# TensorE's order in a decoder step: a scheduler's interleave, or the order of the text

## The chip, the cores and the metric

The kernel runs on one core of one Trainium2 chip. The time is the device time of one launch in microseconds (us), the median of several runs. Each core has a TensorE for matrix products (PE in the profile; its weight loads are PEld), VectorE (DVE) and ScalarE (ACT) for elementwise work, GpSimd (POOL), SyncE (SP), and 16 DMA engines. Each engine runs its own list of instructions in the order in which the built program holds them, and waits for the others by semaphores. So the order in which the instructions of one engine stand is itself part of a kernel.

## The reference

One inference step of a two-layer trunk of width 1024, for a prompt of 1024 tokens and a sample group of 8 x 8 tokens, all in fp32:

```
for layer in (0, 1):
    h = rmsnorm(x)
    layer 0: a_h, a_b, a_c, a_z, shift_in, b_z = split(h @ w_in)
             y_a = a_b * conv3(a_c * a_h) * silu(a_z)
             r, k, v, wl, al = token_shift(shift_in)
             S_t = S_{t-1} * w_t - (S_{t-1} kk_t)(kk_t a_t)^T + v_t k_t^T
             y_b = (group_norm(S_t r_t) + bonus) * silu(b_z)
    layer 1: windowed means with a matrix per group; a gated MLP over chunks of 128 tokens
    x = x + concat(two branches) @ w_out
y = rmsnorm(x)
```

The recurrence S_t has 8 heads of 64 x 64. It is computed in chunks of 64 tokens, by products of 64 x 64 matrices and the inverse of a triangular matrix for each head and chunk.

## The kernel before

The 1088 tokens are the columns of every product. They go in three blocks: block 0 has the 64 sample tokens and 256 of the prompt (320 columns), blocks 1 and 2 have 384 each. Weights come from DRAM in pieces of 128 x 512, and are split into a high part (`whi`, ScalarE, L145) and a low part (`wlo`, VectorE, L146), with 4 buffers of each; activations are split the same way into `hi` and `lo`. A dense product of 1024 inputs and 128 outputs (`product`, L157) is three matmuls for each of 8 steps of 128 inputs: L162 (`hi,whi`), L163 (`lo,whi`) and L164 (`hi,wlo`), 24 in all. I call 12 of them a half: one half uses one piece of the weights. Layer 0 has 33 products of input projection per block (66 halves: 17 products for the recurrence's branch and the gate, then 16 for the convolution branch) and 8 of output projection (16 halves); halves are numbered through the program from 0, and layer 0 has 246.

Between the dense products of layer 0 stand small ones, in three kinds of work per block. *Preparation* (`rwkv_prep`) runs per group of 128 tokens (two chunks), and once for the sample group, nine groups in all: two low-rank products (L487, L488), sums of squares (L496), a spread by transposes (L521), and then on VectorE and ScalarE the decays `Pp`, their inverses `iP`, and the scaled operands. `AR` holds a and r, `BK` holds b and k; in each the second index is the slot. Their products (L555) give `GT`. *Inverse* (`rwkv_inverse`): 31 steps of two VectorE instructions (L610, L612) over all chunks of the block together, and then the result goes through DRAM (L614, L619, L632). *Recurrence* (`recur`): the merge of the inverse's two halves (L639, L651), then for each chunk `chunk_parts` (b and k turned by products with the identity, L692), `rwkv_chunk` (L761 to L788), and for each group the group norm and `group_out` (turned back at L732, result `yr` to DRAM at L739). The output projection (`out_proj0`) reads `yr` from DRAM.

What sets the order. The Tile scheduler orders all engines by its own estimate and by priorities. The kernel bounds it on TensorE: `later()` chains each product behind the one before, `marks` records the last matmul of each half, and `recur` runs its generators (the merge, the chain, the sample, and the preparation of the next block) under `issue_after(marks[...])`, so that a step may start from a certain half on, at 0.7 halves a step (0.5 for the preparation). Where in the dense stream a small product stands from there on is for the scheduler.

Of the kernel before, what the change touches and what calls it, by code (L numbers as in the profile page):

```python
# [8 lines left out]
ALU = mybir.AluOpType  # L9
# [9 lines left out]
AT = (10, 10, 0)  # L19
EARLY, RATE, PREP_RATE = 20, 0.7, 0.5  # L20
# [53 lines left out]
def build(nc, tc, a):  # L74
    from contextlib import ExitStack
    ctx = ExitStack()

# [72 lines left out]
    order, marks = {}, []  # L150

    def later():

        return tc.issue_after(order["last"]) if order else ExitStack()

    def product(ps, w, h, c0, n):

        with later():
            for k in range(KT):
                wh, wl = w[k // 4]  # L160
                hh, hl = h[k]
                mm(ps, wh[:, k % 4, :], hh[:, c0:c0 + n], start=k == 0, stop=False)  # L162
                mm(ps, wh[:, k % 4, :], hl[:, c0:c0 + n], start=False, stop=False)  # L163
                i = mm(ps, wl[:, k % 4, :], hh[:, c0:c0 + n], start=False, stop=k == KT - 1)  # L164
# [61 lines left out]
    def raw_h(B):  # L226
# [32 lines left out]
        with urgent():  # L259
            token_rstd(acc, n, B.ms0, pc, "pp", 4)  # L260
            spread_rstd(B.ms0, n, ev, pc, "pp", "d", XTs[2].rearrange("p a b -> p (a b)"), 4)
            B.rstd = XTs[2].rearrange("p a b -> p (a b)")[:, :n]
            B.rstd2 = XTs[1].rearrange("p a b -> p (a b)")[:, :n]
            act(B.rstd2, B.rstd, AF.Square)
        return h
# [16 lines left out]
    def rms_token(B):  # L282
        B.ms0 = mk(ev, [128, 4], "rms_m", 2)
        with later():
            token_rstd(B.acc, B.n, B.ms0, pd, "dn")

    def rms_spread(B):
        with later():
            B.rstd = spread_rstd(B.ms0, B.n, ev, pd, "dn")
# [175 lines left out]
    def rwkv_prep(B, t0, T, g):  # L465
# [17 lines left out]

        ap, lw = pp(), pp()
        for p in range(4):
            s = slice(p * T, (p + 1) * T)
            mm(ap[:, s], wa2[64:128, p * 128:(p + 1) * 128], B.S28[64:128, cols], start=True, stop=True)  # L487
            mm(lw[:, s], wa2[0:64, p * 128:(p + 1) * 128], B.tw[:, cols], start=True, stop=True)  # L488
        for p in range(4):
            act(sb[:, p], ap[:, p * T:(p + 1) * T].rearrange("p (c s) -> p c s", c=ng_), AF.Tanh,  # L490
                bias=a0h[:, p:p + 1], scale=0.5)
# [37 lines left out]
        for p in range(4):  # L529
            act(g4(kp)[:, p], sb[:, p], AF.Identity, scale=kah[:, p:p + 1], bias=kah1[:, p:p + 1])  # L530
        tt(v3(kp), v3(kp), B.KS[:, :, cols], ALU.mult)
        if g is None:
            stt(sb[:, :, 0, :], sb[:, :, 0, :], 1.0, v3(kkn), ALU.add, ALU.mult)
        else:
            sb2 = sb.rearrange("p a c s -> p (a c) s")
            stt(sb2, sb2, 1.0, kkn.rearrange("p (a s) -> p a s", s=64), ALU.add, ALU.mult)
        yield
        tt(m4(sb), m4(sb), iP, ALU.mult)  # L538
        tt(m4(sa), kv4, Pp[:, :, :, 0:Lc], ALU.mult)
        yield  # L540
        tt(m4(sk), kp.rearrange("p (a c s) -> p a c s", a=4, c=nc_), iP, ALU.mult)
# [4 lines left out]
        for c in range(ng_):  # L546
# [134 lines left out]
    def chunk_parts(B, g, c):  # L681
# [6 lines left out]
        for p in range(4):  # L688
            for q in range(2):
                for e in range(2):  # L690
                    r = slice(64 * e, 64 * e + 64)
                    mm(bps[e][64 * q:64 * q + 64, p * 64:(p + 1) * 64], B.BK[g][r, p, c, q ^ e, :], ident[r, r],  # L692
                       start=True, stop=True)
# [47 lines left out]
    def rwkv_chunk(B, g, c, parts, yps):  # L741
# [23 lines left out]
        first = state.get("y")  # L765
# [615 lines left out]
```

## Time and profile before

| | |
|---|---|
| runs | 1135.46, 1141.45, 1141.25 us, median 1141.25 |
| the profiled execution, its time | 1138.01 us |
| its span | 1136.2 us |
| TensorE busy | 1090.4 us, 96% |
| VectorE, ScalarE, GpSimd busy | 729.5, 491.5, 164.4 us |
| mean granted TensorE clock | 0.967 |

The span is the time from the first to the last instruction, the run has 1.8 us around it. Shares of busy time are means over stretches of different kinds, so the rows below go by stretches and places. A matmul counts as busy also while the clock is granted at half, and while it stands between others that it keeps apart.

### The profile page before, as it was taken

The page shows a single profiled execution, that of the slowest core. Times are in us where ns is not written, and L with a number is a line of the kernel's source. Part 1 is how long each engine was busy: PE and PEld are TensorE (multiplying, and loading weights), DVE is VectorE, ACT ScalarE, POOL GpSimd, SP SyncE. Part 2 cuts the span into 40 slices and gives each one's busy share as a digit, 9 for nine tenths or more (in the row PEclk, how much of TensorE's full clock was granted, in tenths as well). Part 3 has the DMA queues.
Part 4 walks back from the last instruction along what each step waited for, and adds up shares of the span by engine and source line. Part 5 has one row for each costly group of instructions (what it writes and reads, how often), then busy time and mean ns, then how long its engine had stood idle before and what let it go on. Part 6 is the DMA issues. An engine that isn't in the chain of part 4 may idle for free.

```text
span 1136.2 us, 22856 instructions
## 1 busy us (share of the span) xinstructions
PE 1090.4 (96%) x8719; PEld 1003.7 (88%) x8719; DVE 729.5 (64%) x1526; ACT 491.5 (43%) x1017; POOL 164.4 (14%) x282
## 2 busy tenths in 40 slices
PE   7999999999999999999899999999999999999996
PEld 6998999876756899878799889899999999999995
DVE  7878899457632799478797477695373442245456
ACT  6376654365412554666535654464212111133232
POOL 2313343110301212113301011001010100000000
PEclk9999999899966999999999999899999999999998
DMA  8464563554412454535545687775201111112455
GB/s 263 149 212 129 157 206 123 146 157 145 128 58 65 121 189 125 140 104 150 155 152 149 185 242 222 228 254 186 79 21 55 38 48 38 53 41 91 116 154 183
DMA packets 135341, 154.91 MB, mean 136 GB/s; under 512 B 45560, under 2 KB 88696, under 8 KB 135232
## 3 DMA queue, kind: packets, MB, share of 16 engines
q1 hardware_dynamic: 130912, 146.36, 41.8%
q0 software_dynamic: 2256, 5.03, 2.2%
q10 hardware_dynamic: 2064, 2.08, 0.6%
q8 instruction: 68, 1.11, 0.4%
q14 instruction: 41, 0.34, 0.1%
HBM read 127.77 MB, written 25.64 MB: 135 GB/s over the span
## 4 chain that ended last, share of the span: by engine, by line
PE 40%; DVE 5%; DMA 4%; issue 1%; ACT 1%; POOL 1%; SPq 0%; DVEq 0%; ACTq 0%; POOLq 0%
PE dn L162 12%; PE dn L163 12%; PE dn L164 12%; DMA xn<-xd 2%; DVE wlo L146 1%; PE pl L1166 1%; DVE lo L171 1%; PE pl L1230 1%; DMA wraw<-wout 1%; DVE xn L1071 1%; POOL gvs L712 0%; DMA ma<-yd 0%; ACT whi L145 0%; DMA ma<-yr 0%; PE pp L732 0%
## 5 line engine op out<-in xcount | busy, mean ns | idle before, releaser
L162 PE MATMUL dn<-hi,whi 128*128 128x384 f32 (+1 forms) x1648 | 557.4, 338 | 12.9 <-ACT whi L145 6.5
L163 PE MATMUL dn<-lo,whi 128*128 128x384 f32 (+1 forms) x1648 | 551.9, 335 | 0.4 <-DVE lo L171 0.2
L164 PE MATMUL dn<-hi,wlo 128*128 128x384 f32 (+1 forms) x1648 | 551.5, 335 | 0.3 <-DVE wlo L146 0.3
L145 ACT CAST whi<-wraw 128x512 fp32r<-128x512 f32 x326 | 201.0, 619 | 347.1 <-PE dn L163 287.9
L162 PEld LDWEIGHTS dn<-hi,whi 128*128 128x128 f32 x1648 | 314.5, 191 | 25.2 <-ACT whi L145 6.9
L146 DVE TENSOR_TENSOR wlo<-wraw,whi 128x512 fp32r<-128x512 f32 x326 | 223.4, 687 | 159.5 <-ACT whi L145 146.8
L164 PEld LDWEIGHTS dn<-hi,wlo 128*128 128x128 f32 x1648 | 314.4, 191 | 8.5 <-issue 5.6
L163 PEld LDWEIGHTS dn<-lo,whi 128*128 128x128 f32 x1648 | 314.9, 191 | 7.7 <-issue 3.7
L183 POOL TENSOR_TENSOR rms_m<-rms_m,nhalf 128x3 f32<-128x3 f32 (+2 forms) x8 | 6.9, 870 | 218.3 <-DVE rms_m L182 218.3
L555 PE MATMUL pp<-AR,BK 64*64 64x128 f32 x544 | 36.3, 289 | 1.9 <-DVE BK L538 1.6
L555 PEld LDWEIGHTS pp<-AR,BK 64*64 64x64 f32 x544 | 22.0, 138 | 13.9 <-issue 9.8
L612 DVE TENSOR_TENSOR iv<-iv,prod 80x31 f32<-80x31 f32 (+23 forms) x93 | 31.3, 336 | 2.0
L610 DVE TENSOR_TENSOR prod<-iv 80x31 f32<-80x31 f32 (+23 forms) x93 | 31.2, 336 | 1.8
L565 POOL DMA_DIRECT2D dl<-GT x32 | 20.3, 636 | 77.8 <-DVE GT L558 77.8
L712 POOL TENSOR_TENSOR gvs<-gvs,nhalf 128x8 f32<-128x8 f32 (+1 forms) x9 | 15.1, 1674 | 113.0 <-DVE gvs L711 100.6
L1272 DVE TENSOR_TENSOR big<-dn,x1s 128x384 f32<-128x384 f32 (+1 forms) x24 | 12.8, 534 | 27.7 <-PE dn L164 27.7
L558 DVE TENSOR_TENSOR GT<-pp,cst 128x512 f32<-128x512 f32 x34 | 22.1, 683 | 12.3 <-PE pp L555 12.3
L324 POOL COPY q<-carry 128x1 f32<-128x1 f32 x26 | 22.5, 866 | 48.5 <-DVE KS L339 19.7
L1278 ACT ACTIVATE sq<-big 128x384 f32<-128x384 f32 (+1 forms) x21 | 10.7, 508 | 35.1 <-DVE big L1272 35.0
L796 DVE TENSOR_TENSOR pch<-pch,SV 64x256 f32<-64x256 f32 x32 | 13.9, 434 | 17.9 <-PE pch L786 16.3
L500 POOL TENSOR_TENSOR rn<-rn,nhalf 128x8 f32<-128x8 f32 (+1 forms) x9 | 15.5, 1719 | 48.7 <-DVE rn L499 48.7
L326 DVE TENSOR_TENSOR d<-q 128x384 f32<-128x384 f32 (+1 forms) x39 | 20.6, 529 | 1.9 <-ACT q L320 1.5
(279 smaller groups left out, 1246.9 us busy)
## 6 DMA issues: line engine op xcount, KB each, us to landing
wraw<-win SPq DMA_DIRECT2D x246, 256.0 KB, 2.8
wraw<-wout SPq DMA_DIRECT2D x80, 256.0 KB, 3.0
x<-xT SPq DMA_DIRECT2D x48, 192.0 KB, 3.7
xd<-x SPq DMA_DIRECT2D x16, 192.0 KB, 3.1
xn<-xd SPq DMA_DIRECT2D x16, 192.0 KB, 3.9
x1s<-xd SPq DMA_DIRECT2D x16, 192.0 KB, 2.4
yT<-big SPq DMA_DIRECT2D x16, 192.0 KB, 3.7
i<-vd SPq DMA_DIRECT2D x34, 64.0 KB, 2.6
```

The lines of the kernel that those rows point to most:

```text
L145: A.copy(hi, raw)
L146: tt(lo, raw, hi.bitcast(F32), ALU.subtract)
L162: mm(ps, wh[:, k % 4, :], hh[:, c0:c0 + n], start=k == 0, stop=False)
L163: mm(ps, wh[:, k % 4, :], hl[:, c0:c0 + n], start=False, stop=False)
L164: i = mm(ps, wl[:, k % 4, :], hh[:, c0:c0 + n], start=False, stop=k == KT - 1)
L324: G.tensor_copy(q[:, 0:1], carry[:, j:j + 1])
L326: tt(d[:, :n], q[:, 0:n], q[:, 1:1 + n], ALU.subtract)
L555: mm(gp[e][o:o + 64, p * 128:(p + 1) * 128], BK[b:b + 64, p, c, q ^ (e if g is not None else 0), :], AR[b:b + 64, p, c, :, :].rearrange("p ...
L558: tt(GT[:, e::2, :], v3(gp[e]), m[e].unsqueeze(1).broadcast_to([128, 4, 128]), ALU.mult)
L565: nc.gpsimd.dma_start(of_half(B.dl[i], e), GT[64 * e:64 * e + 64, e::2, 0:64])
L610: tt(pr, X[:Q, 0:k, q:q + 1].broadcast_to([Q, k, r]), Lb[:Q, q:q + 1, k:32].broadcast_to([Q, k, r]), ALU.mult)
L612: tt(o, o, pr, ALU.add)
```

## The change

TensorE is taken out of the scheduler's hands (`manual_schedule` for this engine): its instructions stand in the order of the text. The other engines are still ordered by the scheduler. `weave` hands a generator to `half_done`, which `product` calls after each half: each generator has a half from which on it runs, and a rate in halves per step. The start points are in the text of `main`: preparation 27 halves after its block's begin at half a half per step, the recurrences 4, 8 and 4 halves after the place where they are handed over. `finish()` runs what is left.

In the preparation, the value `ta` has its own tile, and `scaled` writes b and k of the odd heads to exchanged slots (`q ^ e`), with two instructions of half the partitions instead of one of all. So in `BK` the stationary operand of a head is one piece of 128 columns: L555 with 64 x 64 operands (16 per chunk) becomes L581 with 64 x 128 (8 per chunk), and L692 becomes 8 transposes (L717).

```diff
+    ctx.enter_context(tc.manual_schedule(engines={mybir.EngineType.PE}))
...
+    def weave(gen, after=0, rate=1.0):
+        streams.append([halves[0] + after, rate, gen])
+    def step(x):
+        with tc.high_priority():
+            if next(x[2], 0) is not None:
+                streams.remove(x)
+        x[0] += x[1]
+    def half_done():
+        halves[0] += 1
+        while streams and (x := min(streams, key=lambda x: x[0]))[0] <= halves[0]:
+            step(x)
...
     def product(ps, w, h, c0, n):
-        with later():
...
-                if k in (3, 7):
-                    marks.append(getattr(i, "ins", i))
-        order["last"] = marks[-1]
+            if k in (3, 7):
+                half_done()
...
+        def scaled(x, q):
+            x = x.rearrange("p (a c s) -> p a c s", a=4, c=nc_)
+            if g is None:
+                tt(m4((sb, sk)[q]), x, iP, ALU.mult)
+            else:
+                for e in range(2):
+                    r, o = slot(e, q)
+                    tt(o, x[r], iP[r], ALU.mult)
...
-                for q in range(2):
-                    for e in range(2):
-                        o, b = 64 * q, 64 * e
-                        mm(gp[e][o:o + 64, p * 128:(p + 1) * 128], BK[b:b + 64, p, c, q ^ (e if g is not None else 0), :],
-                           AR[b:b + 64, p, c, :, :].rearrange("p a s -> p (a s)"), start=True, stop=True)
+                for e in range(2):
+                    r = slice(64 * e, 64 * e + 64)
+                    mm(gp[e][:, p * 128:(p + 1) * 128], BK[r, p, c, :, :].rearrange("p a s -> p (a s)"),
+                       AR[r, p, c, :, :].rearrange("p a s -> p (a s)"), start=True, stop=True)
...
-                    mm(bps[e][64 * q:64 * q + 64, p * 64:(p + 1) * 64], B.BK[g][r, p, c, q ^ e, :], ident[r, r],
-                       start=True, stop=True)
+                PE.transpose(bps[e][:, p * 64:(p + 1) * 64], B.BK[g][r, p, c, :, :].rearrange("p a s -> p (a s)"),
+                             ident[r, r])
...
+    weave(prep(b0), 27, 0.5)
     rwkv_in(b0)
...
+    weave(rwkv_sample(b0), 2)
     mixer_a(b0, hs[0], (3,))
     hs.append(rms_h(b1))
-    at = len(marks)
+    for x in recur(b0):
+        weave(x, 4)
+    weave(prep(b1, b0), 27, 0.5)
     rwkv_in(b1)
...
+    for x in recur(b1):
+        weave(x, 8)
+    weave(prep(b2, b1), 27, 0.5)
     rwkv_in(b2)
     mixer_a(b2, hs[2], range(4))
...
+    for x in recur(b2):
+        weave(x, 4, 0.9)
     out_proj0(b0)
     out_proj0(b1)
-    with boost(mark):
-        recur(b2, at + AT[2])
+    finish()
...
+    weave(layer_norm(), 1)
```

The rest of the diff moves what the two orders need: `rstd` of block 0 becomes a generator, the wait of the sample for its start (`now`) goes, the tiles `ys` and `prod` share a buffer, and the chaining calls `later()` and `issue_after` go from both layers.

Three places show what the order is. First, TensorE, in the input projection of block 1, where the preparation's products of one group stand; `dn` is the dense product's result, `pp` that of the small ones. Before:

```order
L164 MATMUL dn_3183<-hi_2196,wlo_3180 128x384
L555 MATMUL pp_4536<-AR_4447,BK_4446 64x128
L162 MATMUL dn_3183<-hi_2203,whi_3179 128x384
L555 MATMUL pp_4537<-AR_4447,BK_4446 64x128
L163 MATMUL dn_3183<-lo_2204,whi_3179 128x384
```

After:

```order
L178 MATMUL dn_3569<-hi_2209,wlo_3560 128x384
L176 MATMUL dn_3569<-hi_2216,whi_3559 128x384
L177 MATMUL dn_3569<-lo_2217,whi_3559 128x384
L178 MATMUL dn_3569<-hi_2216,wlo_3560 128x384
L581 MATMUL pp_3582<-AR_3439,BK_3438 128x128
L581 MATMUL pp_3583<-AR_3439,BK_3438 128x128
```

Before, most of the 32 products L555 of this group stand singly between dense matmuls; after, the 16 products L581 of a group stand behind each other, after the last matmul of a half (the rows end with the second of them).

Second, VectorE, at the end of the inverse of block 0; `iv` and `prod` are the inverse and its products, `wlo` the low parts of the weights. Before:

```order
L610 TENSOR_TENSOR prod_1346<-iv_1343,iv_1336 80x156
L146 TENSOR_TENSOR wlo_2714<-wraw_2711,whi_2713 128x512
L612 TENSOR_TENSOR iv_1343<-iv_1343,prod_1346 80x26x6
L610 TENSOR_TENSOR prod_1346<-iv_1343,iv_1336 80x135
L612 TENSOR_TENSOR iv_1343<-iv_1343,prod_1346 80x27x5
L610 TENSOR_TENSOR prod_1346<-iv_1343,iv_1336 80x112
L612 TENSOR_TENSOR iv_1343<-iv_1343,prod_1346 80x28x4
L146 TENSOR_TENSOR wlo_2720<-wraw_2717,whi_2719 128x512
L326 TENSOR_TENSOR d_2663<-q_2660 128x384
```

After:

```order
L636 TENSOR_TENSOR prod_1599<-iv_1596,iv_1589 80x112
L638 TENSOR_TENSOR iv_1596<-iv_1596,prod_1599 80x28x4
L636 TENSOR_TENSOR prod_1599<-iv_1596,iv_1589 80x87
L638 TENSOR_TENSOR iv_1596<-iv_1596,prod_1599 80x29x3
L636 TENSOR_TENSOR prod_1599<-iv_1596,iv_1589 80x60
L638 TENSOR_TENSOR iv_1596<-iv_1596,prod_1599 80x30x2
L636 TENSOR_TENSOR prod_1599<-iv_1596,iv_1589 80x31
L638 TENSOR_TENSOR iv_1596<-iv_1596,prod_1599 80x31
L643 COPY iv_1664<-iv_1596 40x1024
L145 TENSOR_TENSOR wlo_2396<-wraw_2393,whi_2395 128x512
L340 TENSOR_TENSOR d_2309<-q_2306 128x384
L353 SCALAR_TENSOR_TENSOR s28_2248<-d_2309,pv_69,q_2306 128x384
```

Before, the inverse's instructions stand between the splits of some twenty weight pieces; after, the last 35 stand in one block behind the split of half 70, and the split for half 71 stands behind them.

Third, TensorE, where the last group of block 2 is turned back (`yc`) and the output product of block 2 follows. Before:

```order
L163 MATMUL dn_8064<-lo_7882,whi_8054 128x384
L164 MATMUL dn_8064<-hi_7881,wlo_8055 128x384
L732 MATMUL pp_8986<-cst_66,yc_8973 64x64 x16
L162 MATMUL dn_8064<-hi_7887,whi_8060 128x384
L163 MATMUL dn_8064<-lo_7888,whi_8060 128x384
```

After:

```order
L177 MATMUL dn_8712<-lo_8092,whi_8708 128x384
L178 MATMUL dn_8712<-hi_8091,wlo_8709 128x384
L757 MATMUL pp_8749<-cst_68,yc_8683 64x64 x16
L176 MATMUL dn_8893<-hi_8835,whi_8883 128x384
L177 MATMUL dn_8893<-lo_8836,whi_8883 128x384
```

Before, the turn stands in the middle of the fourth product of block 1's output projection; after, it stands behind that projection's last matmul, and the next instruction is the first matmul of block 2's.

## Rows read from the trace of the kernel before

**Rows 1.** The page: span, and busy time of each engine.

```profile
span 1136.2 us, 22856 instructions
...
PE 1090.4 (96%) x8719; PEld 1003.7 (88%) x8719; DVE 729.5 (64%) x1526; ACT 491.5 (43%) x1017; POOL 164.4 (14%) x282
```

**Rows 2.** Busy time by stretches: start:end, length, each engine (instructions), clock, DMA.

```profile
22.60:59.60 37.00, 37.00 (x254) 37.00 (x253) 31.93 (x69) 13.93 (x23) 12.62 (x35) 1.00 0.53 167
...
274.00:392.10 118.10, 115.73 (x618) 82.98 (x615) 57.79 (x113) 39.06 (x81) 21.31 (x32) 0.81 0.30 91
...
561.90:620.10 58.20, 58.20 (x337) 58.20 (x337) 49.49 (x115) 24.70 (x45) 8.80 (x16) 1.00 0.54 163
620.10:704.30 84.20, 79.67 (x1256) 71.93 (x1255) 52.49 (x106) 50.16 (x114) 6.33 (x5) 1.00 0.71 209
...
22.60:762.20 739.60, 714.26 (x6453) 637.71 (x6452) 533.65 (x1128) 380.16 (x795) 141.78 (x221) 0.96 0.53 157
...
762.20:1136.20 374.00, 361.66 (x2189) 352.87 (x2187) 180.67 (x359) 96.80 (x192) 17.66 (x37) 0.99 0.28 87
```

**Rows 3.** Stretches again, with instructions of line L162 alone.

```profile
22.60:762.20 739.60, 329.35 (x961) 184.81 (x961) 0.96 0.53 157
...
620.10:704.30 84.20, 32.54 (x96) 18.04 (x97) 1.00 0.71 209
```

**Rows 4.** Span and mean granted clock.

```profile
core 0: 1136.2 us, clock 0.967
```

**Rows 5.** Stretches: the 6.8 us behind the idle time at 723 us.

```profile
727.00:733.80 6.80, 6.71 (x24) 6.07 (x24) 4.69 (x11) 2.84 (x6) 1.30 (x4) 0.50 0.63 209
```

**Rows 6.** TensorE timeline at 331 us: start, length, instruction, count, idle before.

```profile
331.65 0.69 PE L555 MATMUL pp<-AR,BK 64*64 64x128 f32 x2
...
332.88 0.69 PE L555 MATMUL pp<-AR,BK 64*64 64x128 f32 x2
```

**Rows 7.** TensorE timeline at 111 us: a burst of L555 and the dense product behind it.

```profile
110.89 1.97 PE L555 MATMUL pp<-AR,BK 64*64 64x128 f32 x62
112.79 0.42 PE L163 MATMUL dn<-lo,whi 128*128 128x320 f32 x1
```

**Rows 8.** TensorE timelines at 73, 76 and 671 us: L488 pairs, L521, L692.

```profile
72.75 0.27 PE L488 MATMUL pp<-tw,wa 64*128 64x64 f32 x1
...
72.86 0.27 PE L488 MATMUL pp<-tw,wa 64*128 64x64 f32 x1
...
76.33 0.46 PE L521 MATMUL pp<-cst,tm 64*128 64x64 f32 x4
...
671.35 0.69 PE L692 MATMUL pp<-cst,BK 64*64 64x64 f32 x32
```

**Rows 9.** Timeline of all engines at 100 to 110 us: exponential and first L555.

```profile
100.00 0.63 ACT L513 ACTIVATE Pp<-tm 128x512 f32<-128x512 f32 x1
...
109.75 0.43 PE L555 MATMUL pp<-AR,BK 64*64 64x128 f32 x2 [1.27 <-DVE BK L538]
```

**Rows 10.** VectorE groups by line and shape: the scaled copy L538.

```profile
L538 DVE TENSOR_TENSOR BK<-BK,iP 128x512 f32<-128x512 f32 x8 | 5.5, 686 | 0.0
```

**Rows 11.** The page, and timelines at 606 and 622 us: the inverse and its merge.

```profile
L612 DVE TENSOR_TENSOR iv<-iv,prod 80x31 f32<-80x31 f32 (+23 forms) x93 | 31.3, 336 | 2.0
...
606.33 0.21 DVE L612 TENSOR_TENSOR iv<-iv,prod 96x31 f32<-96x31 f32 x1
...
621.99 0.69 PE L639 MATMUL pp<-x,GT 32*32 32x32 f32 x32
```

**Rows 12.** Timelines at 701 to 726 us: the last L732, yr, the product on it.

```profile
701.04 1.15 PE L732 MATMUL pp<-cst,yc 64*64 64x64 f32 x32 [0.25 <-DVE yc L713]
...
706.66 0.54 SPq L739 DMA_DIRECT2D yr<-iP  x1
...
725.75 0.44 PE L162 MATMUL dn<-hi,whi 128*128 128x384 f32 x1 [2.03 <-ACT hi L170]
```

**Rows 13.** TensorE timeline of the start: the token sums.

```profile
15.29 0.78 PE L179 MATMUL pp<-onesc,acc 128*128 128x1 f32 x6
```

More of the change, by code (lines that the diff above doesn't have):

```diff
@@ L148, in weight, with finish @@
         return out
-    order, marks = {}, []
-    def later():
-        return tc.issue_after(order["last"]) if order else ExitStack()
-    def product(ps, w, h, c0, n):
-        with later():
[L159 to L164, printed above, removed]
-                if k in (3, 7):
-                    marks.append(getattr(i, "ins", i))
-        order["last"] = marks[-1]
+    streams, halves = [], [0]
+    def weave(gen, after=0, rate=1.0):
[9 more added lines that the diff above has]
+            step(x)
+    def finish():
+        while streams:
+            step(min(streams, key=lambda x: x[0]))
+    def product(ps, w, h, c0, n):
+        for k in range(KT):
+            wh, wl = w[k // 4]
+            hh, hl = h[k]
+            mm(ps, wh[:, k % 4, :], hh[:, c0:c0 + n], start=k == 0, stop=False)
+            mm(ps, wh[:, k % 4, :], hl[:, c0:c0 + n], start=False, stop=False)
+            mm(ps, wl[:, k % 4, :], hh[:, c0:c0 + n], start=False, stop=k == KT - 1)
+            if k in (3, 7):
+                half_done()
     def split_to(hi, lo, x):
@@ L264, in raw_h @@
             act(B.rstd2, B.rstd, AF.Square)
+        weave(rstd(), 1)
         return h
@@ L944, in rwkv_in, with recur @@
         in_proj_bz(B, hs[B.i])
-    def recur(B, at, nxt=None):
-        done, merged, now = [0], [0], [0]
-        start = at
+    def recur(B):
+        merged = [0]
+        B.done = 0
         def merge():
@@ L982, in chain, with prep @@
             group_out(B, *last)
-        def prep():
-            for q, x in enumerate(nxt.gl):
-                while done[0] < min(q + 1, B.ng):
-                    yield
-                yield from rwkv_prep(nxt, *x)
-                yield
-        streams = [[at, RATE, merge()], [at, RATE, chain()]]
-        if B.i == 0:
-            streams.append([at - EARLY, RATE, rwkv_sample(B, now)])
-        if nxt is not None:
-            rwkv_begin(nxt)
-            streams.append([at, PREP_RATE, prep()])
-        while streams:
-            x = min(streams, key=lambda x: x[0])
-            now[0] = x[0] >= start
-            with (tc.issue_after(marks[int(x[0])]) if x[0] < len(marks) else ExitStack()):
-                if next(x[2], 0) is not None:
-                    streams.remove(x)
-            x[0] += x[1]
-        for p in range(4):
-            ydr[(B.i, 4 + p)] = B.yr[:, p, :]
-    def boost(mark):
-        return tc.high_priority(tc.cur_priority - mark)
+            for p in range(4):
+                ydr[(B.i, 4 + p)] = B.yr[:, p, :]
+        return merge(), chain()
+    def prep(B, before=None):
+        rwkv_begin(B)
+        for q, x in enumerate(B.gl):
+            while before is not None and before.done < min(q + 1, before.ng):
+                yield
+            yield from rwkv_prep(B, *x)
+            yield
+        rwkv_inverse(B)
     b0, b1, b2 = Bs
@@ L1013, in build @@
         V.tensor_scalar(kkbd[:, p, :], C("bd"), kk2[:, p:p + 1], None, ALU.mult)
+    weave(prep(b0), 27, 0.5)
     rwkv_in(b0)
-    rwkv_begin(b0)
-    for x in b0.gl:
-        with urgent() if x[2] is not None else ExitStack():
-            for _ in rwkv_prep(b0, *x):
-                pass
-    rwkv_inverse(b0)
-    mark = tc.cur_priority
     rms_stat(b1)
@@ L1124, in build @@
     v_in((0,), (b1,))
-    with later(), urgent():
+    with urgent():
         norm1(b2)
@@ L1130, in build @@
     ps = mk(pl, [128, 512], "pl", None)
-    with tc.issue_after(order["last"]):
-        mm(ps, ones, ws.rearrange("p g t -> p (g t)"), start=True, stop=True)
+    mm(ps, ones, ws.rearrange("p g t -> p (g t)"), start=True, stop=True)
     for g in range(4):
@@ L1135, in build @@
     ps = mk(pl, [128, 512], "pl", None)
-    with tc.issue_after(order["last"]):
-        mm(ps[:, 0:256], ones[0:64], wss.rearrange("p g t -> p (g t)"), start=True, stop=True)
+    mm(ps[:, 0:256], ones[0:64], wss.rearrange("p g t -> p (g t)"), start=True, stop=True)
     for g in range(4):
```

108 lines of the change are left out of this document (39 added, 69 removed).

## The prediction

> **What bounds the kernel now.** I read the busy shares first, then the table of stretches, then the same table for L162 alone (one in three dense matmuls), the clock, and the timelines of three places. TensorE is busy for 1090.4 of 1136.2 us [rows 1]; no other engine bounds the whole. But "busy" hides two losses, so I set against it what the same work would take without them. A "half" is 12 dense matmuls, four of them from L162.
>
> - Pace. 22.6 to 59.6 us is 21 halves of 320 columns: 37.0/21 = 1.76 us each. 561.9 to 620.1 is 28 halves of 384: 58.2/28 = 2.08 us [rows 2].
> - Dense work of layer 0 after the start: 961 L162 from 22.6 to 762.2 us, 240 halves [rows 3]; block 0 has 60 of its 66 left there and 16 of its output product, blocks 1 and 2 the other 164: 133.8 + 341.1 = 474.9 us.
> - Small products. In the last recurrence, 620.1 to 704.3 us, 96 L162 make 24 halves (16 of 1.76, 8 of 2.08: 44.8 us); TensorE is busy 79.67 us with 1256 records, so 34.9 us go to 1256 - 288 = 968 small records, 36 ns each [rows 2, 3]. There they stand in bursts. A preparation group has 64 records of L555 in 1.9 us [rows 7] and about 40 others at which I put 3.6: 5.5 us, nine groups 50. All of 22.6 to 762.2 has 6453 - 3 x 961 = 3570 small records; the 2625 outside the preparations cost 95. Together 145 us.
>
> Start, dense and small: 22.6 + 474.9 + 145 = 642.5, and layer 0 in fact ends at 762.2. The 120 us over are: idle 739.6 - 714.3 = 25 us [rows 2]; most of what the clock takes, (1 - 0.967) x 1136.2 = 37.5 us over the span [rows 4]; and some 60 us in which small products stand one by one between dense ones. The place to see this is 274 to 392 us: 118.1 us, TensorE busy 115.7, clock 0.81, 618 records where other stretches have twice as many per us [rows 2]. From one lone pair of L555 records to the next, with one dense matmul between, pass 1.23 us at the half clock [rows 6]; the 64 records in one burst took 1.9 us, 0.06 a pair [rows 7]. The scheduler's order does this; the text order of the change puts each set in one piece.
>
> **The change part by part.** (L192, L207, L517, L542, L581, L665 and L757 are lines of the changed kernel; all other lines are of the kernel before.)
> *One-by-one order: gone.* If all 120 us over went and nothing came, layer 0 would end at 642 and the span at 642 + 374 (layer 1 [rows 2]) = 1016. But what the scheduler's freedom bought goes with it: before, a small product that was not ready let dense ones pass. Now TensorE stands still until it is. So the sum is 1016 plus the new stalls.
>
> *Start, +3 us.* The token sums now stand behind the first half, not at 15.29 us [rows 13] behind three and a half. Their operand is complete only then, so some 5 us of waiting come, of which I give back 2, since weights arrive late there anyhow. Bounds 0 and 5.
>
> *Preparation, +39 us.* In each of the nine groups the transposes L542 stand 1.5 halves behind L517 and the products L581 two halves behind L542 (3.5 to 4.2 us). Between L542 and L581 VectorE has seven to nine instructions of 0.69 us [rows 10], two of them new: each odd-head slot is written by two half-height instructions, 16 in all, 11 us of VectorE. That is 4.8 to 6.2 us and no less, so 1 to 2.5 us of stall at best; in the trace of before the exponential stands at 100.00 and the first L555 at 109.75, 9.75 us later, with other work between [rows 9], so 6 at worst. L517 to L542 passes GpSimd's power and a copy on ScalarE behind its other work: 1.5 to 3 us. Per group 2.3 to 9 us, taken 4.3 (nearest the low end, since the streams' elementwise work has high priority): nine groups 39, bounds 21 and 81. What is queued behind: every dense matmul.
>
> *Inverse of block 0, +19 us.* VectorE's row shows it: the inverse's last 35 instructions stand in one block behind a weight split, and the next split, wanted by the next dense half, behind them. 35 x 0.336 [rows 11] and a copy give some 14 us; it begins when TensorE frees a weight buffer, about half 67. From the last one to the merge L639 it took 606.33 to 621.99, 15.5 us [rows 11], through two transfers. The sample's products and L665 stand at halves 70 and 71, five halves of cover, 10.4 us: 14 + 15.5 - 10.4 = 19. Bounds 8 (the block starts earlier) and 25. Before, the same instructions lay between splits and the merge came 20 halves later, hidden.
>
> *Inverses of blocks 1 and 2, +11 us.* The same path, begun earlier against its merge: 6.5 and 4.5. Bounds 0 and 25.
>
> *The last recurrence, +11 us.* The last L757 stands directly ahead of the output product of block 2, which reads yr from DRAM. Before, L732 at 701.04 went ahead, yr left at 706.66 and the first dense product on it began at 725.75 after 2.03 us idle [rows 12]: 24.7 us, much of it reads issued late. At least 5.6 to the store and two transfers, some 13 to 14; one half (2.1) covers. I take 11 more than before; bounds 8 and 20.
>
> *The chain's steps, +12 us.* Sixteen chunks, each step one half behind the last; copies on ScalarE come in between. 0.75 us a chunk; bounds 0 and 25.
>
> *Clock, +12 us.* The 2.03 us of idle at 723 us were followed by 6.8 us at 0.50 of the clock, 727.0 to 733.8 [rows 5, 12]: 3.4 us lost. The stalls of 1.3 us ahead of L555 at 109.75 were not [rows 9]. Five or so of the new stalls reach 2 us by the sum: 12; bounds 0 and 48.
>
> *Turned slots, -2.5 us.* L555 goes from 32 records of 64x64 a chunk to 16 of 64x128. The nearest row of that form, pairs of L487 and L488 on the two row halves, has 0.11 us a pair [rows 8]: 8 x 0.11 = 0.9 a chunk, and 32 records at 1.9/64 are 0.95. Saved 0.05, sixteen times 0.8; were the halves not run together it would cost 14. L692 (32 records, 0.69 [rows 8]) becomes 8 transposes; L521's four in 0.46 are 62 ns apart, 0.5 together: about 2 us over all. Bounds -7 and +14.
> The Trainium skill, "TensorE: Matmul & The Clock Gate", Part 3, has small matmuls in different row and column groups of the array run at the same time, which speaks against this part of the change: the four quarters already ran together. The row of L555 agrees (four records in 0.12 us). By that rule the term is 0; by the count of instructions it would be half of 16 x 0.95, 7.6 us.
>
> *Layer 1, -1.5 us*: the normalisation's products go in groups.
>
> Sum: 3 + 39 + 19 + 11 + 11 + 12 + 12 - 2.5 - 1.5 = 103. Span 1016.5 + 103 = 1119.5; the profiled run is 1138.01 for 1136.2, so 1121.3. The median of the runs, 1141.25, lies 0.28% above that run: 1124.
>
> **Rivals.**
> *The stalls are hidden.* While TensorE stands, VectorE and ScalarE, 64% and 43% busy over the span, get ahead, so that a stall is paid once and not at the next place. For it: in 274 to 392 us VectorE is half idle [rows 2]. Against: at 22.6 to 59.6 us it is busy for 31.9 of 37.0, with the preparations of block 0 still to come. Preparations 21, inverses 15, chain 3, clock 3: the sum falls by some 46 us to 1078.
> *Each preparation waits for its whole chain, and it gets slower.* In-order VectorE serves weight splits, which themselves wait for TensorE's buffers, ahead of the chain; each group then stalls 9 us (9.75 for the chain of before, less 3.5 of cover, and 2.8 ahead of L542): 81 instead of 39, so 1124 + 42 = 1166. It turns to slower at 26 us more, 7.2 a group. For it: 9.75 us [rows 9]. Against: that chain had low priority for its sources there.
> *The clock falls behind every stall.* Fourteen stalls of over 2 us, each with a fall as at 727 us: 48 instead of 12, 1160. For it: rows 5 and 12; against: TensorE is at the full clock through most of the bursts of 620 to 704 us, idle 4.5 us in sum [rows 2].
> The Trainium skill, same page, Part 1, says that idle gaps of the engine bring the clock down; the trace agrees at 723 us.
> *Nothing gained.* Stalls add up to 115 to 125 and eat just what the order gives: about 1140.
>
> **How the numbers follow.** Forecast 1124 (1100 to 1135) 0.46; hidden stalls 0.17; nothing gained 0.13; slower 0.24, of which the preparations 0.16 and the clock 0.08. Less than 0.5% cannot be told from no change here, 1135.5 to 1147: faster 0.63, same 0.13, slower 0.24. The range takes in the hidden case and most of the slower one: 1075 to 1164.
>
> **What would show it.** Right: the one-by-one stretch is gone and the clock there 1.0; TensorE's waits for the operands of L581 lead the list of waits, 2 to 5 us each; one long wait near the first L665 of block 0, 15 to 20 us; one of about 11 us at the last output product; a span of L581 sets near 0.9 us a chunk. Wrong: idle of TensorE in layer 0 under 60 us (the hidden case) or over 130, or a clock below 0.96 with no lone pairs left.

## The result: 8% slower, and the profile after

The changed kernel takes 1230.45 us (1229.52 to 1235.36), 1.0796 times the kernel before [1.0744, 1.0848], where 1124 was forecast. The head of its page, and its mean clock:

```profile
span 1228.8 us, 21517 instructions
...
PE 1078.1 (88%) x8063; PEld 1013.8 (83%) x8063; DVE 749.8 (61%) x1542; ACT 492.5 (40%) x1017; POOL 156.8 (13%) x282
```

```profile
core 0: 1228.8 us, clock 0.932
```

Against [rows 1, 4] the 92.6 us of span come apart like this. TensorE stands still for 1228.8 - 1078.1 = 150.7 us where it was 45.8: 105 more. By its mean the clock takes (1 - 0.932) x 1228.8 = 83.6 us where it took 37.5; but a part of that falls on time in which TensorE stood still anyway. Counted only where it was busy, in pieces of 0.1 us of the trace, the clock takes 57.3 us where it took 32.5: 25 more. What is left, TensorE's work at the full clock, is 1020.9 us where it was 1057.9: 37 *less*. 105 + 25 - 37 = 93. So a gain of the kind that was forecast came; the price for it was higher. All further splits into idle time, clock and work are worked out in this way. By stretches (start:end, length, busy time of each engine, clock; the same places in the program as [rows 2], and three more):

```profile
28.10:817.20 789.10, 684.39 (x5796) 633.20 (x5795) 547.59 (x1138) 380.56 (x794) 132.63 (x217) 0.92 0.49 146
304.70:403.20 98.50, 87.70 (x598) 82.11 (x597) 76.10 (x155) 54.78 (x110) 23.73 (x36) 0.97 0.50 148
192.10:216.00 23.90, 10.47 (x45) 8.60 (x46) 12.50 (x35) 2.94 (x16) 3.37 (x4) 0.50 0.31 73
868.90:935.60 66.70, 51.71 (x253) 46.25 (x253) 33.28 (x87) 4.21 (x10) 5.46 (x11) 0.85 0.06 18
817.20:1228.80 411.60, 377.05 (x2190) 365.03 (x2188) 184.41 (x360) 96.81 (x192) 18.41 (x38) 0.95 0.25 80
```

The first is layer 0 behind the start: 789.1 us against 739.6, idle for 104.7 us against 25.3, clock 0.92 against 0.96. The second answers to the stretch of one-by-one products (halves 90 to 120): 98.5 us, clock 0.97, where 202.0 to 383.2 us were 181.2. The two hold the same dense products but not the same small ones: 1364 TensorE records before, 598 after, 360 of them dense in both. So the difference of 82.7 us is not all gain: 766 small records that now stand elsewhere, at the 49 ns that one takes on average in layer 0 of the kernel before (175.6 us for 3570), are some 38 us of it. The last is layer 1: 411.6 us against 374.0, where I had forecast 372.5. The fourth, halves 270 to 282, alone takes 66.7 us; the kernel before took 38.8 for it. The two stretches of the kernel before:

```profile
202.00:383.20 181.20, 175.76 (x1364) 129.51 (x1362) 91.17 (x174) 77.62 (x176) 24.34 (x34) 0.86 0.39 115
814.40:853.20 38.80, 38.44 (x254) 35.97 (x254) 29.84 (x86) 4.35 (x10) 5.59 (x11) 1.00 0.11 32
```

What TensorE of the changed kernel waited for (total, times, longest):

```profile
PE pp L665 <- DMA x<-dn: 18.4, 4, 10.8
PE pp L581 <- DVE BK L563: 18.2, 10, 4.9
PE pp L861 <- ACT tm L850: 15.5, 1, 15.5
PE pp L542 <- ACT tm L539: 15.3, 5, 6.5
PE pl L1158 <- DVE big L1160: 15.0, 27, 1.9
PE dn L176 <- ACT yst L381: 8.1, 3, 4.6
PE dn L176 <- ACT hi L183: 7.7, 2, 7.4
PE pl L1220 <- DVE big L1210: 7.5, 1, 7.5
```

L665, L581, L861 and L542 are the places that the prediction named. L1158 and L1220 are in layer 1, where it named none. At L861 the timeline shows how the inverse of block 0 holds TensorE up:

```profile
189.53 0.41 DVE L636 TENSOR_TENSOR prod<-iv 80x247 f32<-80x247 f32 x1
...
204.49 0.21 DVE L638 TENSOR_TENSOR iv<-iv,prod 80x31 f32<-80x31 f32 x1
```

```profile
204.73 0.21 ACT L852 COPY prod<-pp 64x64 f32<-64x64 f32 x1 [14.13 <-DVE iv L638]
```

```profile
205.53 0.47 PE L861 MATMUL pp<-cst,tm 64*64 64x64 f32 x2 [15.46 <-ACT tm L850]
...
220.81 1.11 PE L871 MATMUL pp<-tm,xt 64*64 64x64 f32 x16 [2.58 <-DMA xt<-dl]
```

VectorE works the inverse off in one piece to 204.7 us, as its order said. ScalarE's copy L852 into `prod` waits 14.13 us for its end, because `ys` now shares that buffer, and L861's own operand L850 stands behind the copy. L871 then waits for the result by DMA.

### The profile page after: what moved, and what is told of

The parts are those of the page before. It is cut to its first block, busy times and chain, and to the rows that moved or that the text cites. A ratio compares the mean times of both kernels' runs of the same rounds, so it can differ in the third digit from the quotient of the medians.

```text
span 1228.8 us, 21517 instructions
## 1 busy us (share of the span) xinstructions
PE 1078.1 (88%) x8063; PEld 1013.8 (83%) x8063; DVE 749.8 (61%) x1542; ACT 492.5 (40%) x1017; POOL 156.8 (13%) x282
## 4 chain that ended last, share of the span: by engine, by line
PE 39%; DVE 6%; DMA 4%; issue 1%; ACT 1%; POOL 1%; SPq 0%; DVEq 0%; ACTq 0%; POOLq 0%
PE dn L176 12%; PE dn L177 11%; PE dn L178 11%; PE pl L1158 1%; DVE wlo L145 1%; DMA xd<-x 1%; DVE big L1160 1%; DMA xn<-xd 1%; DMA ma<-yr 1%; PE pl L1220 1%; DVE lo L184 0%; ACT whi L144 0%; DVE xn L1065 0%; DVE vh L1146 0%; DVE wp L1200 0%
## 5 line engine op out<-in xcount | busy, mean ns | idle before, releaser
L176 PE MATMUL dn<-hi,whi 128*128 128x384 f32 (+1 forms) x1648 | 571.1, 347 | 24.5 <-ACT yst L381 8.1
L176 PEld LDWEIGHTS dn<-hi,whi 128*128 128x128 f32 x1648 | 321.8, 195 | 37.2 <-ACT yst L381 9.1
L177 PEld LDWEIGHTS dn<-lo,whi 128*128 128x128 f32 x1648 | 322.1, 195 | 5.1 <-DVE lo L184 3.0
L178 PEld LDWEIGHTS dn<-hi,wlo 128*128 128x128 f32 x1648 | 321.4, 195 | 0.2 <-DVE wlo L145 0.2
L581 PE MATMUL pp<-AR,BK 64*128 64x128 f32 x272 | 27.4, 340 | 19.3 <-DVE BK L563 18.2
L581 PEld LDWEIGHTS pp<-AR,BK 64*128 64x128 f32 x272 | 23.6, 239 | 23.6 <-issue 14.8
L925 DVE TENSOR_TENSOR x<-dn,x 128x384 f32<-128x384 f32 (+1 forms) x24 | 12.8, 532 | 24.3 <-PE dn L178 22.4
L1158 PE MATMUL pl<-ws,vh 128*128 128x128 f32 x64 | 14.9, 316 | 12.4 <-DVE big L1160 12.4
L1158 PEld LDWEIGHTS pl<-ws,vh 128*128 128x128 f32 x64 | 10.4, 194 | 17.0 <-DVE big L1160 17.0
L665 PE MATMUL pp<-x,GT 32*32 32x32 f32 x256 | 6.9, 204 | 18.4 <-DMA x<-dn 18.4
```

The costliest lines, as they stand in the source:

```text
L581: mm(gp[e][:, p * 128:(p + 1) * 128], BK[r, p, c, :, :].rearrange("p a s -> p (a s)"), AR[r, p, c, :, :].rearrange("p a s -> p (a s)"), st ...
L1158: mm(mp[:, g * T:(g + 1) * T], vh[:T, g * 128:(g + 1) * 128], rhs, start=True, stop=True)
```

## The experiments

In each, the edit is to the changed kernel unless it says otherwise.

### Layer 1: e1_ln

```diff
             mm(mp[:, g * T:(g + 1) * T], vh[:T, g * 128:(g + 1) * 128], rhs, start=True, stop=True)
+        for g in range(4):
             c = cbs if T == 64 else cb
```

> The changed kernel with one loop cut in two: in ln_b of layer 1 the four matmuls L1158 stand first and the four VectorE reads of their result (L1160) behind them, instead of matmul, read, matmul, read. Theory (text order lets each matmul stand behind the read of the slice before it, because all four write one PSUM tile): the 15.0 us of waits at L1158 and most of the 10 us that the clock lost from 270 to 282 halves go; that stretch falls from 66.7 to about 40 us, the run from 1230.5 to about 1205. Rival (the stretch is long because each of the nine token tiles waits for its own statistics): the wait moves to vh, the stretch stays over 58 us, the run over 1222.

1204.06 us, ratio to the kernel before 1.0549 [1.0532, 1.0565]: 26.4 us back. The theory holds. The timeline of the changed kernel shows the pattern (four products of one token tile, each behind the read of the slice before), and the stretch with the loop cut is as short as it was in the kernel before:

```profile
875.55 0.43 PE L1158 MATMUL pl<-wss,vh 64*128 64x64 f32 x2
877.83 0.43 PE L1158 MATMUL pl<-wss,vh 64*128 64x64 f32 x2 [1.85 <-DVE big L1160]
878.64 0.68 PE L1158 MATMUL pl<-wss,vh 64*128 64x64 f32 x2 [0.38 <-DVE big L1160]
879.70 0.69 PE L1158 MATMUL pl<-wss,vh 64*128 64x64 f32 x2 [0.38 <-DVE big L1160]
```

```profile
871.40:909.20 37.80, 36.53 (x254) 35.89 (x254) 29.70 (x87) 4.15 (x10) 5.41 (x11) 1.00 0.10 28
```

The waits are short (0.38 to 1.85 us), but the clock was 0.85 over the stretch and is 1.00 now: 13.7 us of idle time and 9.6 of clock are gone there. In the kernel before, the same text stood in the scheduler's order, with dense matmuls between the four products.

### The turned slots: e2_slots, e13_half, e8_slots_only, e11_boost_slots

```diff
 e2_slots
-            return r, BK[r, :, :, q ^ e, :]
+            return r, BK[r, :, :, q, :]
...
+            tt(m4((sb, sk)[q]), x, iP, ALU.mult)
...
+                        mm(gp[e][o:o + 64, p * 128:(p + 1) * 128], BK[b:b + 64, p, c, q ^ (e if g is not None else 0), :], ...
... (and the turn by 16 products with the identity)
 e13_half, against e2_slots
+                for e in range(2):
+                    r, o = slot(e, q)
+                    tt(o, x[r], iP[r], ALU.mult)
```

> The changed kernel with the old slots: b and k of all heads written by one instruction each, the products as 64x64 operands (16 a chunk) and the turn by 16 products with the identity, in the same text order. Theory (the four quarters of the array ran together already): TensorE's busy time within 5 us, the run within 1224 to 1236; if anything faster, since VectorE has 11 us less ahead of L581. Rival (half as many instructions are half the time, 7 to 10 us): 1238 or more. Second rival (the two added half-height instructions lie on the path to L581 in all groups): 9 x 1.4 us of waits with the clock behind them go, about 1212.

> The old slots and old products of e2_slots (1221 us) with one part of the turned slots put back: b and k written by two half-height instructions for each group of two chunks instead of one, to the old places. TensorE's order and products are those of e2_slots. If the writes are what the turned slots cost (11 us of VectorE, on the path to L581): 1228 to 1234, as the changed kernel. If it is the form of the products and the turn by transposes: 1216 to 1224, as e2_slots.

e2_slots: 1221.06 us (1213.0 to 1224.12), 1.069 [1.0643, 1.0737]; 9.4 us faster than with the turned slots, between the theory (1224 or more) and the second rival (about 1212), and in the direction of the latter. e13_half: 1230.09 us (1226.79 to 1235.58), 1.0789 [1.0754, 1.0823], as the changed kernel, with the old products. So in this order the half-height writes are the whole price, and the new form of the products is worth nothing that can be measured in the run's time. VectorE's groups for the writes (e2_slots, then e13_half) and TensorE's wait at the products:

```profile
L558 DVE TENSOR_TENSOR BK<-ta,iP 128x512 f32<-128x512 f32 x8 | 5.5, 682 | 0.0
```

```profile
L563 DVE TENSOR_TENSOR BK<-ta,iP 64x512 f32<-64x512 f32 x16 | 10.9, 682 | 0.2
```

```profile
PE pp L577 <- DVE BK L558: 11.6, 6, 3.9
```

```profile
PE pp L582 <- DVE BK L563: 17.3, 12, 4.9
```

An instruction on 64 partitions takes 0.682 us, and so does one on 128: half the height halves nothing. The wait at the products goes from 11.6 to 17.3 us.

e8_slots_only put the turned slots alone into the kernel before:

> The kernel before, with its scheduler's order of TensorE, and the turned slots alone (half-height writes, L555 as 64x128, the turn by transposes). Theory (the four quarters ran together already; VectorE's added 11 us lie beside TensorE's work in that order): within 0.7% of the kernel before, 1134 to 1149. Rival (half the small instructions, each costing 0.4 us where it stands alone between dense matmuls): 1120 or less. Second rival (the 11 us of VectorE cost time here as they did in the text order, 9 us): 1150.

1168.33 us, 1.0238 [1.02, 1.0276], slower than the theory and both rivals said. It separates nothing: the scheduler made another order of the whole layer 0 (halves 90 to 120 took 101 us instead of 181, halves 230 to 246 119 instead of 41). Another pair, e11_boost_slots against e9_boost, stands below.

### The clock: e3_fill, e12_fillall, e7_lone

```diff
 e3_fill
         rq = pp()
+        for _ in range(18):
+            mm(rq[:, 0:512], ident, go_on, start=True, stop=True)
 e12_fillall: the same, and ahead of L542 (2), of the first L581 of a group (3), of the first L665 (7, 12)
```

> The changed kernel with 18 matmuls of 128x512 on constants put ahead of L861, into the PSUM bank that L861 overwrites, so that TensorE works where it stood still for 15.5 us at 190 us (added work, nothing of the output changes). Theory (the clock falls because the engine stands still): the 23.9 us at half clock from 192 to 216 us go, the stretch from half 66 to 72 falls from 47.8 to about 35 us and the run by about 12 to 1218. Rival (the clock falls because the work around there is small products and ScalarE's copies, whatever the engine does in the gap): the low stretch stays and the run stays at 1230 or rises by what the added work is too long.

> The changed kernel with added matmuls of 128x512 on constants ahead of most places where TensorE stands still in layer 0: 2 ahead of each L542, 3 ahead of each group's first L581, 18 ahead of L861, 7 and 12 ahead of the first L665 of blocks 1 and 2 (0.87 us each at the full clock), into banks that are then overwritten. Added work, the waits themselves stay. Theory (most of the clock that layer 0 loses is lost behind idle time): of the 83 us that the clock takes 35 to 40 go, and since the added work is as long as the waits at most places, the run falls by 20 to 35, to 1196 to 1210. Rival (the clock falls as much behind small products as behind idle time): the clock still takes over 65 us and the run stays over 1222.

e3_fill: 1228.63 us, 1.077 [1.0752, 1.0789]. The added work in the gap, and a stretch as long as 192.1 to 216.0 us of the changed kernel, from the start of the added work on:

```profile
189.41 15.61 PE L860 MATMUL pp<-go_on,cst 128*128 128x512 f32 x36
```

```profile
189.40:213.30 23.90, 23.90 (x85) 13.72 (x85) 14.58 (x40) 3.98 (x17) 3.38 (x4) 0.93 0.41 99
```

The added 15.61 us fill the gap, and the clock is 0.93 there instead of 0.50: at this place it fell because TensorE stood still. Yet the run gained 1.8 us, which can't be told from nothing, instead of 12, and the stretch of halves 66 to 72 2.6 (45.3 for 47.8). The 12 were half of the 23.9 us at half clock, and that counts the standing still twice: of the 23.9 us TensorE was busy for 10.5. The clock cost 6.9 us of its work in halves 66 to 72, and costs 3.4 now. e12_fillall: 1231.98 us, 1.0796 [1.0753, 1.0838], mean clock:

```profile
core 0: 1230.3 us, clock 0.959
```

By the mean the clock takes (1 - 0.959) x 1230.3 = 50 us instead of 83.6, near the 35 to 40 less of the theory. Of busy time it takes 27.0 us in layer 0 instead of 44.5: two fifths of layer 0's loss are shown to hang on these gaps, where the theory had said most. The run gained nothing, as the rival said: idle time fell by 55 us there, and the added work is 73, longer than the waits by as much as the clock gave back.

e7_lone puts small products apart again, with no other change:

```diff
             mm(ps, wh[:, k % 4, :], hh[:, c0:c0 + n], start=k == 0, stop=False)
+            lone and lone.pop(0)()
...
+                    lone.append(one) if B.i == 1 else one()
+            while lone:
+                yield
```

> The changed kernel with the products L581 of block 1's three groups put one by one between dense matmuls (48 matmuls, each between two of the dense product), everything else as it was. Theory (a lone small product between dense ones costs 0.4 to 0.5 us at the full clock where one in a burst costs 0.06 to 0.1): 48 x 0.4 = 19 us more, 1250, and the clock may fall there without any idle time, then up to 30 more. Rival (the loss before came from the clock and the waits alone, not from standing apart): 1226 to 1235, since the dense matmuls cover the waits of L581.

1296.52 us, 1.138 [1.1327, 1.1433]: 66 us for 48 matmuls. The same 598 TensorE instructions that took 98.5 us above:

```profile
304.00:462.10 158.10, 140.23 (x598) 109.64 (x597) 74.38 (x144) 55.34 (x110) 24.07 (x36) 0.74 0.31 92
```

59.6 us more: the clock takes 40.0 us of busy time for 3.1, idle time is 17.9 us for 10.8, and 15.7 us are work, 0.33 per lone matmul. So standing apart costs mainly through the clock. Two stretches at half clock, the first in e7_lone, the second in the kernel before:

```profile
324.40:355.10 30.70, 30.08 (x75) 20.99 (x76) 12.28 (x22) 6.58 (x14) 2.60 (x4) 0.50 0.29 91
```

```profile
324.20:354.90 30.70, 30.70 (x79) 16.00 (x78) 5.22 (x8) 2.95 (x5) 3.56 (x6) 0.50 0.10 26
```

In e7_lone the clock is at half three times, for 30.7, 27.3 and 23.9 us, while the lone products run, and each time it has fallen behind a wait of 4.2 to 4.6 us. The changed kernel has the first of these waits too, and there the clock was back after 3.4 us. So here the lone products hold the clock down; that it also falls without such a wait the kernel before shows, whose TensorE never stood still for over 1.0 us between 285 and 388 us. Lone products alone are not enough, though: those from 277 to 311 us ran at the full clock. Over all of layer 0 behind the start the written order takes 42 us of TensorE's work away (682.1 before, 639.9 after), but the clock takes more than before (44.5 us for 32.0): what is saved on lone products is lost again behind waits.

### The places of the stalls: e4_prate, e5_delay, e10_ys, e6_best

```diff
 e4_prate
-    weave(prep(b1, b0), 27, 0.5)
+    weave(prep(b1, b0), 27, 0.8)
-    weave(prep(b2, b1), 27, 0.5)
+    weave(prep(b2, b1), 27, 0.8)
 e5_delay
-    weave(rwkv_sample(b0), 2)
+    weave(rwkv_sample(b0), 12)
...
-        weave(x, 4) / weave(x, 8) / weave(x, 4, 0.9)           (blocks 0, 1, 2)
+        weave(x, 14) / weave(x, 14) / weave(x, 8, 0.75)
 e10_ys: the copies into ys stand behind the copy into r2
```

> The changed kernel with the preparation of blocks 1 and 2 woven at 0.8 halves a step instead of 0.5, so that L542 stands 2.4 halves behind L517 and L581 3.2 behind L542. Theory (the stall at L542 and L581 is the elementwise chain less the cover): the waits there, about 3 + 12 us in blocks 1 and 2, and the falls of the clock behind them, about 12 us, shrink to a third; the merges wait a few us longer because the inverse begins later; 1230 falls to about 1212. Rival (what is gained there is lost again at the merges L665, since the inverse's end sets them): 1230 or more, with L665 waiting over 30 us.

> The changed kernel with later starts: the sample's recurrence 12 halves behind its place instead of 2, the recurrences 14, 14 and 8 halves instead of 4, 8 and 4, the last at 0.75 halves a step instead of 0.9. Theory (the merges stand too near to the inverses' ends): the waits at L861 (15.5 us), L871 (2.6) and L665 (18.4) go nearly all, with some 30 us of clock behind them; 1230.5 falls to about 1180. Rival (the elementwise engines are late by themselves, so that the wait moves along to the later place or to the next preparation): 1215 or more, L665 still waiting over 12 us.

> The changed kernel with the sample's copies into ys (which shares the buffer of the inverse's products) moved behind the copies into r2, so that L861 no longer waits for the end of the inverse by way of that buffer. Theory (two waits stand on one producer: without the first, TensorE waits at L871 for the inverse that comes back by DMA): the 15.5 us at L861 go, 8 to 12 come at L871, the run gains 3 to 10 us, 1221 to 1227. Rival (the shared buffer alone makes the stall): the stretch of halves 66 to 72 falls from 47.8 to 20 us and the run by over 20 us.

e4_prate: 1262.18 us, 1.1067 [1.1046, 1.1087], 32 slower; the rival. The preparation ends later, the inverse with it, and TensorE waits at the merge:

```profile
PE pp L665 <- DMA x<-dn: 45.5, 4, 23.8
PE pp L581 <- DVE BK L563: 24.6, 8, 4.9
```

e5_delay: 1223.89 us, 1.0728 [1.0685, 1.0772], 7 faster; the rival, though L665 waits 11.8 us and not over 12. L861's wait has shrunk from 15.5 to 3.0 us, and others have grown:

```profile
PE pp L581 <- DVE BK L563: 22.9, 8, 8.8
PE pp L542 <- ACT tm L539: 18.7, 6, 6.2
...
PE pp L665 <- DMA x<-dn: 11.8, 2, 10.9
...
PE pp L871 <- DMA xt<-dl: 6.1, 1, 6.1
```

e10_ys: 1234.64 us, 1.0833 [1.0785, 1.0881], 4 slower, which the intervals don't part from no change. The wait at L861 is gone; the one for the same inverse behind it (L871, here L876) took its place and more. The theory had the mechanism, and a gain of 3 to 10 us that didn't come:

```profile
PE pp L876 <- DMA xt<-dl: 24.5, 1, 24.5
```

e6_best adds up the later starts, the cut loop, the old slots, the last pool product of layer 1 one dense product later, and block 0's preparation at 0.75:

> All repairs in one: the loop of ln_b cut in two, the last pool_out of layer 1 one dense product later, the old slots, the later starts, and the preparation of block 0 at 0.75 halves a step. If the single terms add up: 1230.5 - 26.4 (ln_b) - 9.4 (slots) - 11 (pool_out: a wait of 7.5 us at L1220 and 3 to 4 us of clock) - 50 (later starts) - 15 (preparation of block 0, half of its stalls) = 1119, below the kernel before. Rival (the stalls stand in for each other: what is taken from one place comes at the next): 1141 or more.

1167.19 us, 1.0239 [1.0204, 1.0274]. 63 us come back of the 111 expected. By stretches of halves, layer 1 gives 39 (28.9 at ln_b, 11.4 at the pool product, as expected), block 0's preparation 18 (halves 27 to 66). All of layer 0 from half 66 on gives 9 us, the old slots' part included, so the later starts give nearly nothing of the 50: in layer 0 the stalls move on to other places, in layer 1 they are gone.

### The same gain in the scheduler's order: e9_boost, e11_boost_slots

e9_boost is the kernel before with one number changed. The scheduler mixed small and dense products where their priorities met:

```diff
     def boost(mark):
-        return tc.high_priority(tc.cur_priority - mark)
+        return tc.high_priority(tc.cur_priority - mark + 1500)
```

> The kernel before with one number changed: the priority that lifts the recurrence's work over the dense products is raised by 1500 more, so that in the scheduler's order of TensorE the small products of a set stand together (6 lone ones between halves 90 and 120 instead of 90); old slots, old layer 1. Theory (the loss of the kernel before lies in products that stand apart and in the clock that falls there, and the scheduler's order has few stalls otherwise): halves 90 to 120 take 100 to 110 us instead of 181, little is lost elsewhere, the run falls from 1141 to 1070 to 1095. Rival (the scheduler's order pays for whatever it gains with stalls in another place, as the text order did): over 1125.

> The raised priority of e9_boost together with the turned slots (half-height writes, products of 64x128, turns by transposes), in the scheduler's order. Theory (the turned slots save TensorE under 4 us and cost VectorE 11): 0 to 10 us slower than e9_boost. Rival (fewer instructions in a burst save 8 us or more): faster than e9_boost by 6 us or more.

1096.2 us (1092.52 to 1101.24), 0.9609 [0.9569, 0.9648]: faster than both kernels. Its clock, the stretch of halves 90 to 120, and the longest waits but the first:

```profile
core 0: 1095.3 us, clock 0.979
```

```profile
203.90:346.70 142.80, 133.49 (x1416) 111.20 (x1416) 98.10 (x199) 78.41 (x178) 28.00 (x39) 0.96 0.53 151
```

```profile
PE pp L577 <- DVE GT L558: 3.9, 4, 1.6
PE pch L761 <- issue: 2.9, 2, 2.1
```

Idle time is 47 us, as before; no wait behind the start is over 2.1 us. The clock takes 18.9 us of busy time for 32.5, and the work is 1029.5 for 1057.9. So the gain of bursts can be had without the stalls. The stretch can be compared with the kernel before, which has about as many small products in it (1364 records, here 1416): 142.8 us for 181.2, with 5.1 us for 25.3 lost to the clock and 128.3 for 150.5 of work. These 38 us are nearly the whole gain of the span, 40.9. The stretch fell less than forecast (100 to 110), and the run ended 1 us above its range (1070 to 1095). The raised priority acts on all engines, so what the other engines' new order adds is not separated.

e11_boost_slots, the same with turned slots, takes 1120.78 us, 0.9831 [0.9796, 0.9866]: 24.6 us slower than e9_boost, where 0 to 10 was expected. Its span is 23.3 us longer, with 14.1 us more idle, 7.8 more of clock and 1.3 more of work: on TensorE the turned slots save nothing here. How much of the added idle time and clock is theirs, and how much the scheduler's other order, stays open.

## Why the prediction was wrong

The mechanisms were right in both directions, and the idle time nearly so; layer 1, the clock and the floor (the work that was to be left) were off, all on the same side: 39, 33 and 22 us. With 13 us of idle time and 2 at the start they make the 109 us by which the span of 1119.5 was missed.

| term | forecast, us | measured, us |
|---|---|---|
| layer 0 behind the start, work at the full clock | 617 (floor less 2.5) | 639.9 |
| start, longer by | 3 | 5.5 |
| idle time of layer 0 behind the start | 92 | 104.7 |
| of it: L542, L581 | 39 | 34.6 |
| of it: inverse of block 0 (L861, L871) | 19 | 18.1 |
| of it: merges of blocks 1, 2 (L665) | 11 | 18.4 |
| of it: last recurrence | 11 | 7.4 |
| of it: steps of the chains (L796, L717, L896) | 12 | 13.7 |
| clock in layer 0 | 12 | 44.5 |
| turned slots | -2.5 | +9.4 (mostly in the waits at L581; part of the rows above) |
| layer 1 | -1.5 | +37.6 |

*Clock, the step that failed first.* "Five or so of the new stalls reach 2 us by the sum: 12." In layer 0 it took 44.5 us. I counted stalls by their mean length; but the waits at L542 reach 6.5 us, those at L581 4.9, that at L861 15.5. In layer 0 behind the start the trace has 17 waits of 2.0 us or more, not five or so, and a stretch at half clock in or close behind each of them (16 stretches, two waits share one; one more, of 3.4 us, has no such wait ahead). A stretch took 2.6 us of busy time on average, less than the 3.4 that I had put: the count failed, not the price. The rival that priced this at 48 us, for fourteen stalls, was right in its size, and got a chance of 0.08. e3_fill shows the link at one place, e12_fillall for two fifths of the loss; for the rest it is only seen side by side. The sign that I had named, a clock below 0.96 with the lone pairs gone, came.

*Layer 1.* "The normalisation's products go in groups" was read off the kind of work, not off the order. Product, read, product, read of one PSUM tile stands in the text as four waits: 26.4 us (e1_ln). Another 11 come at L1220, where the text puts the pool product directly behind its windows: without that (e6_best) layer 1 takes 372.3 us, what I had forecast.

*The floor.* Counted from each matmul's start to the next one's, at the full clock and without idle time, the small products took 143.0 us, as forecast (145 - 2.5); the dense ones took 496.9, not 474.9. Dense matmuls between dense ones kept the pace (2659 of them, 0.165 us each). Those next to a small product or ahead of a wait, 221, cost 22 us more, as here in the changed kernel, where the first behind L703 takes 0.26 us to the next start and the others 0.17 to 0.18:

```profile
187.39 0.60 PE L703 MATMUL pp<-cst,BK 128*128 128x128 f32 x4
187.74 0.42 PE L176 MATMUL dn<-hi,whi 128*128 128x384 f32 x1
188.00 0.34 PE L177 MATMUL dn<-lo,whi 128*128 128x384 f32 x1
188.18 0.34 PE L178 MATMUL dn<-hi,wlo 128*128 128x384 f32 x1
188.35 0.34 PE L176 MATMUL dn<-hi,whi 128*128 128x384 f32 x1
```

The floor had no term for going from dense to small and back, which a burst pays once and a lone product each time. So the products that stood apart before cost not some 60 us of work but 42 (682.1 in layer 0 behind the start, 639.9 now). The reading that other stretches have twice as many records per us as the one-by-one stretch holds for the last recurrence alone, not for the two dense stretches [rows 2].

*Turned slots.* I priced the products, and put VectorE's 11 us inside the stalls of the preparation without adding it. e13_half shows that these writes are on the path, 9 us, and that the products save nothing in the run's time.

*Right.* The loss of the kernel before: e7_lone makes it, e9_boost takes it away. The stalls, by place; that their five parts add up to 92.2 us where 92 was forecast is in part luck, since the merges were 7 us over and the preparations and the last recurrence 8 under. The other 12.5 us of idle time are at places that the prediction hadn't named, 8.1 of them where dense products wait for ScalarE's L381, the gate of the input projection. At the inverse of block 0 the block on VectorE was right, the link was not: the shared buffer of `ys` came first, the DMA behind it. The size was luck: without the shared buffer the way through the DMA, which the 19 us priced, takes 24.5 (e10_ys).

What stays open: what makes the clock fall where TensorE is busy and its products stand apart (the kernel before shows that it does, not why), what the three fifths of layer 0's clock loss that e12_fillall left hang on, and how much of e11's 24.6 us is the slots' own.

## What to carry to other kernels

An order that keeps small products together is worth much here, but an order that can't step aside pays for every operand that is late, and pays again in clock: price a stall of TensorE as its length and the fall behind it. Before an engine is taken out of a scheduler's hands, look for one number that makes the scheduler group: here a raised priority gave 3.9% and the written order cost 8.0%. When order is text, write all matmuls into one PSUM tile before the reads of it.

## What the runs showed of the hardware

- A VectorE instruction on 64 partitions took as long as one on 128: 0.682 us for the same 512 columns.
- 48 small matmuls set singly between dense ones cost 1.24 us each, 0.33 of it work and the rest mostly by the clock, with TensorE busy for 140 of 158 us. Behind the same wait of 4.6 us the clock stayed at half for 30.7 us with lone products and for 3.4 us without.
- With waits of 0.4 to 1.9 us at L1158 the clock was 0.85 over 66.7 us with 15 us of idle time, and 1.00 when they were gone. I had expected short waits to be free, from the 1.3 us ahead of L555 [rows 9].
- A dense matmul took 0.165 us to the next one's start inside a dense stretch, and 0.28 us as the first behind a small product (107 of them in layer 0).
- Added matmuls in a gap held the clock at 0.93 where it had been 0.50, and did not pay: over the gaps filled by e12_fillall, 73 us of added work took away 55 us of idle time and gave back 17 us of clock.
